# Prompt attention in groups of query blocks: scores, V products and transposes as runs of one shape, and PSUM split 3 and 5

## The chip, the cores and the metric

One core of a Trainium2 chip runs the whole program in one launch. The metric is the device time of one execution in microseconds (us); the kernel before takes 2353.92 us, the median of 3 runs (2352.94 to 2354.88).

## The reference, cut to what matters

One layer of a hybrid decoder is computed for a prompt of 1024 tokens and for 8 sample tokens. RMSNorm and one wide projection give the queries, keys and values of a dilated attention in three groups (windows 128, 512, 2048; dilations 1, 4, 16; 8 heads of 64), the inputs of an mLSTM, and gates. The two branches are gated, merged and projected; a convolutional FFN follows. The part that is changed is the prompt attention of one group:

```
def _dilated_attn_prompt(q, k, v, bias_g, window, dil):
    qb = to_blocks(q)                 # 128 queries of one residue modulo dil
    kb = with_prev(to_blocks(k))      # the block itself and the one before it
    vb = with_prev(to_blocks(v))
    s = jnp.einsum('brnqhc,brnkhc->brnhqk', qb, kb).astype(jnp.float32) * (Dh ** -0.5) + bias
    s = jnp.where(mask[None, None, :, None], s, -jnp.inf)
    lse = jax.nn.logsumexp(s, axis=-1)
    p = jnp.exp(s - lse[..., None]).astype(v.dtype)
    o = jnp.einsum('brnhqk,brnkhc->brnqhc', p, vb)
```

The outputs of the three groups are combined with weights from their log-sums. All data is float32.

## The kernel before, in words

The program runs in phases: norm and transposition of the input; attention (4 pairs of heads, for each the three groups g = 0, 1, 2: twelve units); the mLSTM, four heads; merging and output projection; the FFN. Large projections go through `proj` (L200) and `mm` (L183): a weight of 128 columns is split into a high and a low part (`split`, L175: ACT writes whi at L176, DVE writes wlo at L177), and for each of three token chunks 24 matmuls (L189) accumulate into a PSUM bank. These banks come from the pool `pp` (4 banks); ACT or DVE then empties the bank ("evacuation"). All other PSUM results come from the pool `px` (4 banks) by `X(...)`. Large SBUF tiles come from one pool, `ap_`, with NA = 17 buffers, by `A(...)`.

One attention unit (`attn_unit`, L324) projects q, k and v for 128 columns (two heads), transposes v and k (L365, tile ptr), writes the cache outputs, loads two bias tiles (bt), and goes through eight query blocks. For a block with a previous block nk = 2, else 1: in g = 0 all but the first have one (15 key blocks in all), in g = 1 every second (12), in g = 2 none (8). `stage_s(b)` issues the scores of the two heads, each into a bank of its own (L413, tile s; the heads lie on partitions 0 to 63 and 64 to 127, array shape 64\*128), then for each head a DVE pass that adds the bias and takes the row minimum (L420) and an ACT exponential (L424). `stage_t(b)` transposes the 2·nk blocks of probabilities into one bank (L434, tile pt, shape 128\*128) and copies it to SBUF (L436, tile pts; the planner picks DVE or ACT). `stage_v(b)` multiplies by the values (L451, tile po, shape 128\*64, the two heads on two halves of the columns); after four blocks the po bank is copied to oT (L459 or L463). The loop at L465 issues s of block x, t of block x-1, v of block x-2.

This is program order only. A planner that models time orders each engine's instructions: of what is ready in its model it takes what stands first in the program. So matmuls L189 of the next unit's projections fill places where the attention has to wait ("fillers" here). `in_order(m)` forbids that m moves ahead of the instruction traced before it on its engine; it doesn't forbid others between the two. At run time each engine's order is fixed; semaphores make it wait.

From the second pair on, the units also carry work of the pair before: `combine_b` and `sample_b` after g = 0, `combine_c` (L514) and `sample_c` after g = 1, `sample_d` after g = 2. `combine_c` loads factors (fbc, by the queue of POOL) and multiplies with them on DVE (L519, held in program order); `sample_c` multiplies small matrices on PE (L557, L562, L563), followed by DVE L565 and ACT L566. The gate projection L621 stands after the first unit.

Of the kernel before, what the change touches and what calls it, by code (L numbers as in the profile page):

```python
# [8 lines left out]
F32 = mybir.dt.float32  # L9
# [18 lines left out]
EPS = 1e-6  # L28
BIG = 1e30
NMC = 8  # L30
NA = 17
NF = 16
NC0 = 8

# [6 lines left out]
def kernel(  # L41
# [42 lines left out]

    wk = Phase()
    wk.next()
    pp = ctx.enter_context(tc.tile_pool(name="pp", bufs=4, space=bass.MemoryType.PSUM))
    px = ctx.enter_context(tc.tile_pool(name="px", bufs=4, space=bass.MemoryType.PSUM))

    def A(name, cols=T, dt=F32):  # L90
        return ap_.tile([128, cols], dt, tag="A", name=name)
# [6 lines left out]
    def X(name):  # L98
        return px.tile([128, 512], F32, tag="x", name=name)
# [224 lines left out]
    def attn_unit(pair, g, st):  # L324
        d = DIL[g]
        U = S // d
        qT, kT, vT = A("qT"), A("kT"), A("vT")
        evacs = []
        for kind, dst in enumerate((qT, kT, vT)):
            def evac(ci, t0, n, ps, kind=kind, dst=dst):  # L330
                npm = min(n, S - t0)
                if g == 0:
                    dv, sv = dst[:, t0:t0 + npm], ps[:, 0:npm]
                else:
                    dv = dst[:, 0:S].rearrange("p (r u) -> p r u", r=d)[:, :, t0 // d:(t0 + npm) // d]
                    sv = ps[:, 0:npm].rearrange("p (u r) -> p r u", r=d)
                if kind == 0:
                    nc.scalar.mul(dv, sv, -0.125)
                elif kind == 1:
                    nc.scalar.copy(dv, sv)  # L340
                else:
                    nc.vector.tensor_copy(dv, sv)  # L342
                if npm < n:
                    if kind == 0:
                        nc.vector.tensor_scalar(out=smp[:, pair, kind, g, :], in0=ps[:, npm:n], scalar1=-0.125, scalar2=None, op0=ALU.mult)
                    else:
                        nc.vector.tensor_copy(smp[:, pair, kind, g, :], ps[:, npm:n])
            col = kind * AQ + g * 512 + pair * 128
            if pair == 0 and g == 0 and kind < 2:
                evacs.append(evac)  # L350
                if kind == 1:
                    for ci in range(len(CHUNKS)):
                        for k in range(2):
                            proj_chunk(first_w[k], hT, evacs[k], ci)
            else:
                proj(w_in2[:, col:col + 128], hT, evac)
        vn = A("vn")
        kn = A("kn")
        keep = ((7,), (1, 3, 5, 7), tuple(range(8)))[g]
        for src, dst, blks in ((vT, vn, tuple(range(8))), (kT, kn, keep)):  # L360
            for b0 in range(0, len(blks), 4):
                bl = blks[b0:b0 + 4]
                pt = X("ptr")
                for i, b in enumerate(bl):
                    nc.tensor.transpose(pt[:, i * 128:(i + 1) * 128], src[:, b * 128:(b + 1) * 128], ident)  # L365
                if dst is vn or g != 1:
                    dv = dst[:, bl[0] * 128:(bl[-1] + 1) * 128]
                    sv = pt[:, 0:len(bl) * 128]
                else:
                    dv = dst[:, 0:S].rearrange("p (r n c) -> p r n c", n=2, c=128)[:, :, 1, :]  # L370
                    sv = pt.rearrange("p (r c) -> p r c", c=128)
                if dst is vn:
                    nc.vector.tensor_copy(dv, sv)
                else:
                    nc.scalar.copy(dv, sv)
        for kv, src in ((0, kn), (1, vn)):
            o = kvp[g][0, 0].rearrange("t k h c -> t k (h c)")[:, kv, pair * 128:(pair + 1) * 128]
            if g == 0:
                dma_out(o, src[:, 7 * 128:8 * 128])
            elif g == 1:  # L380
                dma_out(o.rearrange("(u r) c -> u r c", r=4), src[:, 0:S].rearrange("p (r n c) -> p r n c", n=2, c=128)[:, :, 1, :])
            else:
                ov = o.rearrange("(u j q) c -> q u j c", j=8, q=2)
                for q in range(2):
                    dma_out(ov[q], src[q * 64:(q + 1) * 64, 0:S].rearrange("p (j c) -> p j c", c=128))
        bias = []
        for hd in range(2):
            gh = g * 8 + pair * 2 + hd
            bt = wk.tile([128, 256], F32, tag="bias", name="bt", bufs=4)
            r, h0 = (0, 0) if gh < 2 else (1, 2) if gh < 8 else (g + 1, g * 8)  # L390
            base = (gh - h0) * 128 * 384
            if g < 2:
                dma_in(bt, _bcast(rep_d[r][:, :, :], base + 127, [[383, 128], [1, 256]]))
            else:
                dma_in(bt[:, 128:256], _bcast(rep_d[r][:, :, :], base + 255, [[383, 128], [1, 128]]))
                nc.gpsimd.memset(bt[64:128, 128:192], BIG)
            bias.append(bt)
        oT = A("oT")
        live = {}
        pos = [None, None]  # L400

        def span(b):
            prev = (g == 0 and b > 0) or (g == 1 and b % 2 == 1)
            nk = 2 if prev else 1
            return nk, b - (nk - 1)

        def stage_s(b):
            nk, k0 = span(b)
            kw = nk * 128
            ss_ = [X("s"), X("s")]  # L410
            for hd in range(2):
                pr = slice(hd * 64, (hd + 1) * 64)
                m = nc.tensor.matmul(ss_[hd][:, 0:kw], qT[pr, b * 128:(b + 1) * 128], kT[pr, k0 * 128:k0 * 128 + kw], start=True, stop=True)  # L413
                if hd:
                    in_order(m)
            for hd in range(2):
                sb = wk.tile([128, 256], F32, tag="sb", name="sb", bufs=4)
                cm = (g * 8 + b) * 4 + hd
                cl = (g * 8 + b) * 4 + 2 + hd
                nc.vector.tensor_tensor_reduce(  # L420
                    out=sb[:, 0:kw], in0=ss_[hd][:, 0:kw], in1=bias[hd][:, 256 - kw:256], scale=1.0, scalar=3e38,
                    op0=ALU.add, op1=ALU.min, accum_out=st[:, cm:cm + 1],
                )
                nc.scalar.activation(out=sb[:, 0:kw], in_=sb[:, 0:kw], func=ACTF.Exp, scale=-1.0, bias=st[:, cm:cm + 1], accum_out=st[:, cl:cl + 1])  # L424
                live[(b, hd)] = sb

        def stage_t(b):
            nk, _ = span(b)
            pt = X("pt")
            for hd in range(2):  # L430
                p = live.pop((b, hd))
                for i in range(nk):
                    c = (hd * nk + i) * 128
                    nc.tensor.transpose(pt[:, c:c + 128], p[:, i * 128:(i + 1) * 128], ident)  # L434
            pts = wk.tile([128, 512], F32, tag="pts", name="pts", bufs=3)
            nc.any.tensor_copy(pts[:, 0:nk * 256], pt[:, 0:nk * 256])  # L436
            live[b] = pts

        def stage_v(b):
            nk, k0 = span(b)  # L440
            pts = live.pop(b)
            half, bi = divmod(b, 4)
            if bi == 0:
                pos[half] = X("po")
            po = pos[half]
            for i in range(nk):
                kb = k0 + i
                for hd in range(2):
                    pr = slice(hd * 64, (hd + 1) * 64)
                    c = (hd * nk + i) * 128  # L450
                    m = nc.tensor.matmul(  # L451
                        po[pr, bi * 128:(bi + 1) * 128], vn[:, kb * 128 + hd * 64:kb * 128 + hd * 64 + 64],
                        pts[:, c:c + 128], start=(i == 0), stop=(i == nk - 1),
                    )
                    if hd or i:
                        in_order(m)
            if bi == 3:
                if g == 0:
                    nc.any.tensor_copy(oT[:, half * 512:(half + 1) * 512], po)  # L459
                else:  # L460
                    hr = d // 2
                    dv = oT[:, 0:S].rearrange("p (u r) -> p r u", r=d)[:, half * hr:(half + 1) * hr, :]
                    nc.any.tensor_copy(dv, po.rearrange("p (r u) -> p r u", r=hr))  # L463

        for x in range(8 + 2):  # L465
            if x < 8:
                stage_s(x)
            if 0 <= x - 1 < 8:
                stage_t(x - 1)
            if 0 <= x - 2 < 8:  # L470
                stage_v(x - 2)
        return oT

    def combine_a(pair, st):
# [975 lines left out]
```

## Time and profile before

| | before |
|---|---|
| median of 3 runs | 2353.92 us (2352.94 to 2354.88) |
| the profiled execution, its own time | 2352.78 us |
| its span, first to last instruction | 2350.9 us |
| PE (matmul) busy | 2321.8 us, 99% |
| DVE, ACT, POOL busy | 1161.4, 695.9, 212.3 us |
| granted TensorE clock, mean | 0.998 |
| attention phase, about | 67 to 667 us of the span |

In the timeline a row is a merged stretch of equal instructions: start, duration, engine, source line, operation, tiles, array shape (rows\*columns that the instruction uses), operand shape, count, and in brackets the idle time before it with what ended it. A float32 matmul shows as two records, a float32 transpose as one. PEld is the weight load.

### The profile page before, as it was taken

To read this page: it belongs to the slowest core of one execution; us is meant where nothing else is said; L and a number is where in the kernel's file an instruction comes from. 1 tells how busy PE (TensorE), PEld (TensorE's weight loads), DVE (VectorE), ACT (ScalarE), POOL (GpSimd) and SP (SyncE) were. 2 spreads that over 40 slices of the span, in tenths; PEclk is the share of its full clock that TensorE was granted. 3 is DMA by queue.
4 is the path that set the end of the run, shared out by engine and by line. 5 is a ranking of instruction groups with operands and counts; after the bars stand their busy time and mean duration, and the time that the engine had idled before them with its cause. 6 is when DMAs were issued, how large, how long until landed. Compare 5 with 4: busy or idle time off the path is not lost.

```text
span 2350.9 us, 36526 instructions
## 1 busy us (share of the span) xinstructions
PE 2321.8 (99%) x15077; PEld 2185.2 (93%) x15077; DVE 1161.4 (49%) x2697; ACT 695.9 (30%) x1345; POOL 212.3 (9%) x380
## 2 busy tenths in 40 slices
PE   7999999999999999999999999999999999999997
PEld 7888888888889999999999999999999999999997
DVE  6343434324345282827332254346556566655666
ACT  4333333333332332323332221333212222222222
POOL 1112111110120011111121200000000000000000
PEclk9999999999999999999999999999999999999999
DMA  5312433323354142424233631222111111111112
GB/s 175 100 51 75 116 84 89 97 68 95 99 164 130 43 136 59 133 62 133 61 119 88 218 114 46 69 85 63 37 45 44 39 54 54 55 45 38 53 37 77
DMA packets 243015, 196.82 MB, mean 84 GB/s; under 512 B 24392, under 2 KB 220088, under 8 KB 242833
## 3 DMA queue, kind: packets, MB, share of 16 engines
q1 hardware_dynamic: 206577, 124.65, 18.4%
q0 software_dynamic: 36272, 69.84, 9.7%
q8 instruction: 119, 1.95, 0.3%
q14 instruction: 47, 0.39, 0.1%
HBM read 160.30 MB, written 39.20 MB: 85 GB/s over the span
## 4 chain that ended last, share of the span: by engine, by line
PE 93%; issue 3%; DMA 2%; DVE 1%; ACT 1%; POOL 1%; DVEq 0%; SPq 0%; POOLq 0%; ACTq 0%
PE pp L189 67%; PE ppd L1343 10%; PE s L413 3%; PE po L451 2%; PE pt L434 2%; PE pcm L960 1%; PE ni L954 1%; DMA fbc<-f_d 1%; PE ptr L365 1%; PE sm L941 1%; PE na L957 1%; PE pxo L1211 1%; POOL out_dram L108 0%; DMA araw<-aT_d 0%; PE pkm L930 0%
## 5 line engine op out<-in xcount | busy, mean ns | idle before, releaser
L189 PE MATMUL pp<-act_hi,whi 128*128 128x352 f32 (+1 forms) x3272 | 604.8, 324 | 1.3 <-ACT act_hi L241 1.3
L189 PE MATMUL pp<-act_lo,whi 128*128 128x352 f32 (+1 forms) x3272 | 594.2, 321 | 0.0
L189 PE MATMUL pp<-act_hi,wlo 128*128 128x352 f32 (+1 forms) x3272 | 581.5, 319 | 1.1 <-DVE wlo L177 1.1
L189 PEld LDWEIGHTS pp<-act_hi,whi 128*128 128x128 f32 x3272 | 527.6, 188 | 14.6 <-issue 7.7
L189 PEld LDWEIGHTS pp<-act_lo,whi 128*128 128x128 f32 x3272 | 526.9, 188 | 5.8 <-issue 2.2
L189 PEld LDWEIGHTS pp<-act_hi,wlo 128*128 128x128 f32 x3272 | 524.2, 187 | 4.2 <-DVE wlo L177 1.4
L177 DVE TENSOR_TENSOR wlo<-wraw,whi 128x1024 fp32r<-128x1024 f32 (+2 forms) x153 | 182.0, 1190 | 457.8 <-PE pp L189 237.9
L176 ACT CAST whi<-wraw 128x1024 fp32r<-128x1024 f32 (+2 forms) x153 | 156.7, 1024 | 679.8 <-PE pp L189 627.3
L1344 DVE TENSOR_TENSOR x<-x,ppd 128x352 f32<-128x352 f32 (+4 forms) x248 | 124.8, 516 | 75.2 <-PE ppd L1343 75.1
L1269 DVE TENSOR_TENSOR fu<-pp,sq 128x320 f32<-128x320 f32 (+1 forms) x130 | 64.7, 511 | 182.0 <-PE pp L189 181.7
L1343 PE MATMUL ppd<-fhi,dhi 128*128 128x352 f32 (+3 forms) x528 | 124.2, 320 | 2.1 <-DVE yn L1304 2.1
L1343 PE MATMUL ppd<-flo,dhi 128*128 128x352 f32 (+3 forms) x528 | 123.7, 320 | 0.0
L1343 PE MATMUL ppd<-fhi,dlo 128*128 128x352 f32 (+3 forms) x528 | 123.7, 320 | 0.0
L1283 DVE SCALAR_TENSOR_TENSOR y<-fu,fcv,y 128x1048 f32<-128x1048 f32 x88 | 115.1, 1308 | 2.4 <-ACT y L1281 1.2
L424 ACT ACTIVATE sb<-sb,st 128x128 f32<-128x128 f32 (+1 forms) x192 | 85.2, 445 | 42.5 <-DVE st L420 41.4
L1343 PEld LDWEIGHTS ppd<-fhi,dhi 128*128 128x128 f32 x528 | 89.6, 188 | 3.9 <-issue 2.6
L1343 PEld LDWEIGHTS ppd<-flo,dhi 128*128 128x128 f32 x528 | 89.6, 188 | 1.3
L1343 PEld LDWEIGHTS ppd<-fhi,dlo 128*128 128x128 f32 x528 | 89.4, 188 | 1.4
L420 DVE CUSTOM_DVE_ANT_0 sb<-s,bt 128x128 f32<-128x128 f32 (+1 forms) x192 | 61.6, 350 | 51.3 <-PE s L413 41.5
L105 POOL DMA_DIRECT2D gfin<-in_final_norm_g_dram x1 | 0.5, 530 | 911.4 <-DVE fu L1269 911.4
L413 PE MATMUL s<-kT,qT 64*128 64x128 f32 (+1 forms) x384 | 70.8, 370 | 0.0
L342 DVE COPY vT<-pp 128x352 f32<-128x352 f32 (+1 forms) x36 | 18.5, 514 | 105.4 <-PE pp L189 105.4
(380 smaller groups left out, 2386.6 us busy)
## 6 DMA issues: line engine op xcount, KB each, us to landing
wraw<-in_w_in_dram SPq DMA_DIRECT2D x84, 512.0 KB
wraw<-in_w_up_dram SPq DMA_DIRECT2D x44, 512.0 KB
draw<-in_w_down_dram SPq DMA_DIRECT2D x22, 512.0 KB
c<-in_state_mlstm_C_dram SPq DMA_DIRECT2D x32, 256.0 KB
out_dram<-c POOLq DMA_DIRECT2D x32, 256.0 KB, 3.6
qb<-sn_d POOLq DMA_DIRECT2D x12, 512.0 KB, 5.1
kt<-in_cache_kv_w_dram SPq DMA_DIRECT2D x12, 512.0 KB
vt<-in_cache_kv_w_dram SPq DMA_DIRECT2D x12, 512.0 KB
```

The lines of the kernel that those rows point to most:

```text
L176: a = nc.scalar.copy(hi[:, 0:n], raw[:, 0:n])
L177: b = nc.vector.tensor_tensor(out=lo[:, 0:n], in0=raw[:, 0:n], in1=hi[:, 0:n].bitcast(F32), op=ALU.subtract)
L189: nc.tensor.matmul(ps[0:m, 0:n], wt[:, i * m:(i + 1) * m], act[i][which][:, t0:t0 + n], start=(pi == 0 and i == 0), stop=(pi == 2 and i == ...
L413: m = nc.tensor.matmul(ss_[hd][:, 0:kw], qT[pr, b * 128:(b + 1) * 128], kT[pr, k0 * 128:k0 * 128 + kw], start=True, stop=True)
L420: nc.vector.tensor_tensor_reduce(out=sb[:, 0:kw], in0=ss_[hd][:, 0:kw], in1=bias[hd][:, 256 - kw:256], scale=1.0, scalar=3e38, op0=ALU.add ...
L424: nc.scalar.activation(out=sb[:, 0:kw], in_=sb[:, 0:kw], func=ACTF.Exp, scale=-1.0, bias=st[:, cm:cm + 1], accum_out=st[:, cl:cl + 1])
L434: nc.tensor.transpose(pt[:, c:c + 128], p[:, i * 128:(i + 1) * 128], ident)
L451: m = nc.tensor.matmul(po[pr, bi * 128:(bi + 1) * 128], vn[:, kb * 128 + hd * 64:kb * 128 + hd * 64 + 64], pts[:, c:c + 128], start=(i == ...
L1269: nc.vector.tensor_tensor(out=u[:, 2 + t0:2 + t0 + npm], in0=ps[:, 0:npm], in1=r2[:, t0:t0 + npm], op=ALU.mult)
L1283: nc.vector.scalar_tensor_tensor(out=y, in0=u[:, i:i + YW], scalar=fcv3[:, i, j:j + 1], in1=y, op0=ALU.mult, op1=ALU.add)
L1343: nc.tensor.matmul(ps[:, 0:n], wds[j][w][:, m * 128:(m + 1) * 128], parts[j][a][:, t0:t0 + n], start=(x == 0), stop=(x == len(seq) - 1))
L1344: nc.vector.tensor_tensor(out=x1[m][:, t0:t0 + n], in0=x1[m][:, t0:t0 + n], in1=ps[:, 0:n], op=ALU.add)
```

## The change

Query blocks are taken in groups (`groups`, two blocks for g = 0 and 1, four for g = 2). Each stage takes a whole group: the scores of all its blocks go into two banks (one for each head, up to 512 columns), the transposes fill one or two banks of four, and V products follow each other; `chained` holds the matmuls of a stage in program order. Within the transposes the order is reversed, last block first. The loop issues s of group x, v of group x-2, t of group x-1 (V products now stand before the transposes). The bias pass and the exponential stay one for each block and head. PSUM is split 3 (`pp`) and 5 (`px`); sb has 8 buffers instead of 4, and NA is 16 instead of 17. Cut to its core:

```diff
-NA = 17
+NA = 16
...
-    pp = ctx.enter_context(tc.tile_pool(name="pp", bufs=4, space=bass.MemoryType.PSUM))
-    px = ctx.enter_context(tc.tile_pool(name="px", bufs=4, space=bass.MemoryType.PSUM))
+    pp = ctx.enter_context(tc.tile_pool(name="pp", bufs=3, space=bass.MemoryType.PSUM))
+    px = ctx.enter_context(tc.tile_pool(name="px", bufs=5, space=bass.MemoryType.PSUM))
...
+        G = 4 if g == 2 else 2
+        groups = [range(b, b + G) for b in range(0, 8, G)]
+
+        def chained(ms):
+            for i, m in enumerate(ms):
+                if i:
+                    in_order(m)
+
+        def stage_s(bs):
             ss_ = [X("s"), X("s")]
...
+            def matmuls():
+                for b in bs:
+                    nk, k0 = span(b)
+                    kw = nk * 128
+                    for hd in range(2):
+                        pr = slice(hd * 64, (hd + 1) * 64)
+                        yield nc.tensor.matmul(ss_[hd][:, at[b]:at[b] + kw], qT[pr, b * 128:(b + 1) * 128], kT[pr, k0 * 128:k0 * 128 + kw], start=True, stop=True)
+
+            chained(matmuls())
...
+                    sb = wk.tile([128, 256], F32, tag="sb", name="sb", bufs=8)
...
+        def stage_t(bs):
+
+            work = [(b, hd, i) for b in bs for hd in range(2) for i in range(span(b)[0])]
+            banks = [work[i:i + 4] for i in range(0, len(work), 4)]
+            pts = {}
+
+            def matmuls():
+                for bank in reversed(banks):
+                    pt = X("pt")
+                    for x, (b, hd, i) in reversed(list(enumerate(bank))):
+                        yield nc.tensor.transpose(pt[:, x * 128:(x + 1) * 128], live[(b, hd)][:, i * 128:(i + 1) * 128], ident)
+                    t = wk.tile([128, 512], F32, tag="pts", name="pts", bufs=3)
+                    n = len(bank) * 128
+                    nc.any.tensor_copy(t[:, 0:n], pt[:, 0:n])
...
+            chained(matmuls())
...
+        def stage_v(bs):
+            pts = live.pop(bs)
+
+            def matmuls():
+                for b in bs:
...
+                    for i in range(nk):
+                        kb = k0 + i
+                        for hd in range(2):
+                            pr = slice(hd * 64, (hd + 1) * 64)
+                            yield nc.tensor.matmul(
+                                po[pr, bi * 128:(bi + 1) * 128], vn[:, kb * 128 + hd * 64:kb * 128 + hd * 64 + 64],
+                                pts[(b, hd, i)], start=(i == 0), stop=(i == nk - 1),
+                            )
+
+            chained(matmuls())
...
-        for x in range(8 + 2):
-            if x < 8:
-                stage_s(x)
-            if 0 <= x - 1 < 8:
-                stage_t(x - 1)
-            if 0 <= x - 2 < 8:
-                stage_v(x - 2)
+        n = len(groups)
+        for x in range(n + 2):
+            if x < n:
+                stage_s(groups[x])
+            if 0 <= x - 2 < n:
+                stage_v(groups[x - 2])
+            if 0 <= x - 1 < n:
+                stage_t(groups[x - 1])
```

## Rows read from the trace of the kernel before

**Rows 1.** The profile's page, part 1: busy time, share, instructions.

```profile
PE 2321.8 (99%) x15077; PEld 2185.2 (93%) x15077; DVE 1161.4 (49%) x2697; ACT 695.9 (30%) x1345; POOL 212.3 (9%) x380
```

**Rows 2.** Timeline of PE, steady stretch of g = 0.

```profile
237.02 0.70 PE L413 MATMUL s<-kT,qT 64*128 64x256 f32 x4
237.66 0.66 PE L434 MATMUL pt<-ident,sb 128*128 128x128 f32 x4
238.24 0.66 PE L451 MATMUL po<-pts,vn 128*64 128x128 f32 x8
238.83 0.70 PE L413 MATMUL s<-kT,qT 64*128 64x256 f32 x4
```

**Rows 3.** Timeline of PE: longer and shorter stretches.

```profile
96.09 1.09 PE L451 MATMUL po<-pts,vn 128*64 128x128 f32 x16
...
286.70 0.44 PE L434 MATMUL pt<-ident,sb 128*128 128x128 f32 x2
...
287.65 0.49 PE L413 MATMUL s<-kT,qT 64*128 64x128 f32 x4
...
297.28 0.83 PE L557 MATMUL psb<-ohs,rbx 33*16 33x129 f32 x6
```

**Rows 4.** Windows (units): length; PE, PEld, DVE, ACT, POOL busy (x); clock; DMA.

```profile
227.95:245.15 17.20, 17.11 (x131) 10.46 (x130) 12.11 (x52) 10.60 (x37) 3.96 (x8) 1.00 0.73 216
279.47:299.65 20.18, 20.02 (x132) 12.09 (x132) 9.57 (x40) 11.39 (x38) 6.48 (x9) 1.00 0.80 198
334.33:349.05 14.72, 14.72 (x99) 9.29 (x98) 7.53 (x42) 9.46 (x38) 5.21 (x8) 1.00 0.51 127
```

**Rows 5.** Timeline of DVE, then ACT: one block's softmax and copy.

```profile
239.67 0.42 DVE L420 CUSTOM_DVE_ANT_0 sb<-s,bt 128x256 f32<-128x256 f32 x1 [0.43 <-PE s L413]
...
240.37 0.69 DVE L436 COPY pts<-pt 128x512 f32<-128x512 f32 x1
...
240.14 0.51 ACT L424 ACTIVATE sb<-sb,st 128x256 f32<-128x256 f32 x1 [0.24 <-DVE st L420]
```

**Rows 6.** Timeline: start of the program, and the first unit.

```profile
37.92 0.32 PE L189 MATMUL pp<-act_hi,whi 128*128 128x352 f32 x1
...
43.02 0.59 PE L189 MATMUL pp<-act_hi,wlo 128*128 128x352 f32 x2
...
42.38 0.47 ACT L338 ACTIVATE qT<-pp 128x352 f32<-128x352 f32 x1
...
79.74 1.45 PE L189 MATMUL pp<-act_hi,whi 128*128 128x352 f32 x8
...
91.35 0.56 DVE L621 TENSOR_SCALAR gsb<-pp,gb_sb 8x352 f32<-8x352 f32 x1
```

**Rows 7.** Timeline at the end of g = 1, second and third pair.

```profile
281.95 2.52 POOL L105 DMA_DIRECT2D fbc<-f_d  x3
...
301.83 2.36 DVE L519 TENSOR_TENSOR oT<-oT,fbc 128x1024 f32<-128x1024 f32 x2 [6.27 <-DMA fbc<-f_d]
...
462.12 2.36 DVE L519 TENSOR_TENSOR oT<-oT,fbc 128x1024 f32<-128x1024 f32 x2 [9.46 <-DMA fbc<-f_d]
...
464.98 0.62 ACT L566 ACTIVATE ssb<-ssb,s 16x387 f32<-16x387 f32 x1 [8.07 <-DVE s L565]
...
465.60 0.79 ACT L338 ACTIVATE qT<-pp 128x352 f32<-128x352 f32 x2
...
466.22 1.44 PE L189 MATMUL pp<-act_hi,whi 128*128 128x352 f32 x8
```

**Rows 8.** Timeline of PE, then DVE, in the FFN.

```profile
1632.72 1.45 PE L189 MATMUL pp<-act_hi,whi 128*128 128x352 f32 x8
...
1640.16 0.48 PE L1343 MATMUL ppd<-fhi,dhi 128*128 128x352 f32 x2
...
1633.68 1.25 DVE L1316 TENSOR_TENSOR y<-y 128x1048 f32<-128x1048 f32 x1
...
1638.40 0.52 DVE L1269 TENSOR_TENSOR fu<-pp,sq 128x352 f32<-128x352 f32 x1
```

More of the change, by code (lines that the diff above doesn't have):

```diff
@@ L405, in span @@
             return nk, b - (nk - 1)
-        def stage_s(b):
-            nk, k0 = span(b)
-            kw = nk * 128
-            ss_ = [X("s"), X("s")]
[L411 to L447, printed above, removed]
-                for hd in range(2):
[L449 to L453, printed above, removed]
-                    )
-                    if hd or i:
-                        in_order(m)
-            if bi == 3:
+        G = 4 if g == 2 else 2
@@ new lines, in attn_unit @@
+        groups = [range(b, b + G) for b in range(0, 8, G)]
[4 more added lines that the diff above has]
+        def stage_s(bs):
+            ss_ = [X("s"), X("s")]
+            at, c = {}, 0
+            for b in bs:
+                at[b] = c
+                c += span(b)[0] * 128
+            def matmuls():
[6 more added lines that the diff above has]
+            chained(matmuls())
+            for b in bs:
+                kw = span(b)[0] * 128
+                for hd in range(2):
+                    sb = wk.tile([128, 256], F32, tag="sb", name="sb", bufs=8)
+                    cm = (g * 8 + b) * 4 + hd
+                    cl = (g * 8 + b) * 4 + 2 + hd
+                    nc.vector.tensor_tensor_reduce(
+                        out=sb[:, 0:kw], in0=ss_[hd][:, at[b]:at[b] + kw], in1=bias[hd][:, 256 - kw:256], scale=1.0, scalar=3e38,
+                        op0=ALU.add, op1=ALU.min, accum_out=st[:, cm:cm + 1],
+                    )
+                    nc.scalar.activation(out=sb[:, 0:kw], in_=sb[:, 0:kw], func=ACTF.Exp, scale=-1.0, bias=st[:, cm:cm + 1], accum_out=st[:, cl:cl + 1])
+                    live[(b, hd)] = sb
@@ new lines, in stage_t @@
+        def stage_t(bs):
[10 more added lines that the diff above has]
+                    nc.any.tensor_copy(t[:, 0:n], pt[:, 0:n])
+                    for x, w in enumerate(bank):
+                        pts[w] = t[:, x * 128:(x + 1) * 128]
+            chained(matmuls())
+            for b in bs:
+                for hd in range(2):
+                    live.pop((b, hd))
+            live[bs] = pts
@@ new lines, in stage_v @@
+        def stage_v(bs):
+            pts = live.pop(bs)
+            def matmuls():
+                for b in bs:
+                    nk, k0 = span(b)
+                    half, bi = divmod(b, 4)
+                    if bi == 0:
+                        pos[half] = X("po")
+                    po = pos[half]
+                    for i in range(nk):
+                        kb = k0 + i
+                        for hd in range(2):
+                            pr = slice(hd * 64, (hd + 1) * 64)
[4 more added lines that the diff above has]
+            chained(matmuls())
+            for b in bs:
+                half, bi = divmod(b, 4)
+                if bi < 3:
+                    continue
+                po = pos[half]
```

## The prediction

> **What bounds the kernel now.** The page's first part shows PE busy 99% of the span, DVE 49%, ACT 30% [rows 1]: the end is set by what PE spends, and a microsecond that PE is spared is gained as long as PE finds other work ready. I then read the timeline of PE through the attention, where the rows are shortest. In a steady stretch of g = 0 one block's s, t and v take 1.81 us (237.02 to 238.83) [rows 2]. How much of this is work? Rows of the same kind and different length tell: 128 columns more lengthen four score records by 0.70 - 0.49 = 0.21; two transposes more add 0.66 - 0.44 = 0.22, so 0.11 each; eight V records more add 1.09 - 0.66 = 0.43, so 0.054 each [rows 2, 3]. Work is then 0.42 + 0.44 + 0.43 = 1.29, and 0.52 is left, paid once for each stretch of one array shape: some 0.17 at every change between 64\*128, 128\*128 and 128\*64. That is what the reader is to see: PE is busy all the time, yet 0.52 of 1.81 us is no work.
>
> The windows over three units of the second pair say what this sums to. Each window runs from the first scores to the projection behind the last V product: 17.20, 20.18 and 14.72 us [rows 4]. Work by the prices above: g = 0 has 15 key blocks, so 15 x 0.21 for s, 30 transposes x 0.11, 60 V records x 0.054, in all 9.7 us; g = 1 has 12, 7.75; g = 2 has 8, 5.2. In the timeline of PE I counted 9, 13 and 11 filler matmuls at 0.155 (48 of them from 1632.72 to 1640.16 [rows 8]), 1.4, 2.0 and 1.7 us, and small matmuls of the sample tokens, none, 15 and 6 at about 0.12 (0.83 / 6 with its tail [rows 3]), 1.8 and 0.7. What is left is 6.1, 8.6 and 7.1 us. The same timeline has 30, 41 and 38 stretches of one shape: 0.2 each. g = 1 and 2 have more than three for a block, because the planner alternates single transposes with pairs of V records.
>
> **The change part by part.** *Groups, chained.* g = 0 and 1 go from eight trios of stretches to four, g = 2 to two: 10 trios per pair x 0.52 = 5.2 us. Fillers beside transposes have their shape and cost no change; I allow three per unit that do, 0.2 each: 1.8. The sample matmuls keep their own changes, some 1.8 in g = 1 and 2. Sum 8.8 in place of 21.8: 13 per pair, by unit 3.4, 4.9 and 4.7, and 52 over four pairs. The first unit has fewer changes than its fellows (25 stretches from 66.9 to 97.1), so I take 50. The work itself, the passes on DVE and ACT and the DMAs with their queues (SP, POOL) stay as they are.
>
> *Softmax of a group.* This isn't shown before; I build it from rows. The first pass of DVE may have to wait for the last score of the group, as it reads the bank that PE still writes. Two passes take 0.70 on DVE, an exponential 0.5 on ACT, a copy 0.69 [rows 5]. In g = 0 a group needs 4 x 0.35 + 2 x 0.69 = 2.8 of DVE and 4 x 0.5 = 2.0 of ACT against 2 x 1.29 + 0.52 = 3.1 of PE, and from s of a group to its t there is s, v, t of neighbours in between, some 4 us for a chain of 0.14 + 0.35 + 2.0 + 0.2. So it is hidden in the steady part. V of a group now comes right behind one s run of 4 x 0.21 + 0.17 = 1.0 us after the transposes it needs: two copies on two engines (0.69 and a wait) are done by then, on one engine (1.4) they would show 0.4 in each of 40 groups, 16 us at most. At either end of a unit the planner must put fillers; they are the same matmuls as before. Cost taken: nothing; if the fillers don't fit, see the first rival.
>
> *px from 4 to 5.* Two s banks, two pt, one po: one group fits. A gain that I can't price beyond the above; zero.
>
> *pp from 4 to 3.* It bites where a fourth chunk runs before the first is emptied. At the start a fourth chunk runs from 37.92 to 43.02 while the first bank is emptied only at 42.38 [rows 6]; with three banks nearly its whole 24 x 0.155 = 3.7 us moves behind. In the first unit a fourth chunk starts at 79.74 behind three gate chunks that are emptied from 91.35 on [rows 6]; it fills up to 3.8 us in which the attention waits for its softmax. Bounds 0 (if the planner empties sooner) to 7.5; the rows show both holes, so I take 5. In the FFN a chunk that ends where the next eight matmuls begin, at 1632.72, is emptied by 1638.40 + 0.52 = 1638.92, and with three banks it would be due at 1640.16 [rows 8]: 1.2 us of room, cost nothing.
>
> *NA from 17 to 16, sb from 4 to 8.* In the second pair three loads fbc are issued together [rows 7], so several buffers are free where most tiles live at once; cost nothing, upper bound the 0.155 x 24 = 3.7 us of one chunk per pair that can't be emptied, 15.
>
> *What the shorter units run into.* The fbc loads are issued at the start of g = 1 (281.95) and land 20 us later; DVE, in order, sits idle for them 6.27 us in the second pair and 9.46 in the third [rows 7]. They will not land sooner. Behind the waiting L519 stand DVE's L565, behind that ACT's L566 (8.07 us idle), behind that the evacuation L338 of the next q chunk, done near 466.05; PE starts its fourth chunk at 466.22 [rows 7]. With three banks that start can't be earlier: in the third pair the 4.9 us of g = 1 are given back whole. In the other two pairs the idle is 3.2 us shorter, and 1.7 each is given back: 8.3 in all. If the planner puts L565 ahead of L519, since psc is ready sooner, nothing is. Bounds 0 to 3 x 4.9 = 14.7; I take 4, half of 8.3.
>
> **The sum.** -50 + 5 + 4 = -41 us. The profiled execution took 2352.78 us (its span 2350.9), the median of the runs 2353.92, 1.1 more. 2353.9 - 41 = 2313 us.
>
> **The rivals.** *Softmax sets the pace* (2328). DVE and ACT are busy 12.1 and 10.6 of 17.2 us in g = 0 [rows 4]. If no filler fits between a group and its neighbours, a unit lasts as long as its chain: first s 1.1, pass and wait 0.5, then 16 exponentials of 0.5 (g = 0), then t, copy, v 2.7: 12.3 us. With 0.4 for half the columns, an estimate, g = 1 comes to 10.8 and g = 2 to 10.6. Sum 33.7 against 52.1 - 5.1 (fillers, done elsewhere) - 2.5 (sample) = 44.5: 10.8 less per pair, 43; 1 us of latency at each of twelve seams leaves 31. With the holes at the start 2353.9 - 31 + 5 = 2328. For it: DVE is at 70% already. Against: PE was never without fillers. The Trainium skill says the same in TensorEngine Tiling (Array Packing), section PSUM Bottleneck: tiles speed TensorE up, not the emptying of PSUM, and copies may become the bottleneck. The windows don't bear it out yet: no unit is as short as its DVE time.
>
> *The factors hold the attention itself* (2347). If the planner also puts the last pts copies of g = 1 on DVE behind L519, PE's last V products wait until fbc has landed: from 279.47 to 301.8, three multiplications 3.6, copy 0.7, V 1, so 28 us for 20.2, in three pairs 23.4 lost instead of 14.7 gained. 2313 - 4 + 38 = 2347. Against: before, ACT did such copies in that place.
>
> *The runs are split again* (2338). `chained` forbids moving ahead, not standing between; if one of two s banks is late, or the planner puts fillers inside, half of the saved changes return: 25.
>
> *Slower, by the FFN* (2370). The 22 second-half projections have 1.2 us of room [rows 8]. If DVE's order slips by three passes of 1.25 us (L1316 [rows 8]) ahead of the evacuation, each waits 3.75 - 1.2 = 2.6 us, 57 in all: 2313 + 57 = 2370. It decides from a slip of 1.2 us on, and makes the kernel slower from 3.1 us on (41 / 22 + 1.2). For it: DVE is busiest there. Against: the planner knows of the three banks.
>
> **How the numbers follow.** Forecast 0.52 (2313, by itself 2302 to 2325); better, with neither holes nor factors, 0.12 (2304); softmax 0.12; factors 0.06; split again 0.08; nothing changes, since splits and holes eat all, 0.04; slower by the FFN 0.06. From no change a measurement can tell some 0.2%, 4.7 us. So faster 0.90, same 0.04, slower 0.06. The range goes from 2299 (all of the 52, px worth 3 more) to 2338.
>
> **What would show it.** The timeline of a unit of g = 0 should have s rows of eight records, t of eight, V of 16, some 15 to 18 stretches; the windows of the three units should be near 14, 15.5 and 10 us with as many fillers, and a pair's period 13 us shorter. Holes of 3 us should stand near 40 and 80 us. DVE's idle before L519 should grow to some 10 to 14 us. I am wrong if PE has idle rows inside the units, if stretches stay near 100 per pair, or if the projections in FFN or mLSTM lose pace (0.155 per matmul).

## The result, and the profile after

The changed kernel takes 2314.91 us (median of 4 runs, 2312.85 to 2316.65) against 2353.43 (4 runs, 2350.08 to 2354.88): ratio 0.9838, 95% interval 0.9821 to 0.9855, 38.5 us less. The forecast was 2313, 41 less. The profiled execution took 2312.85 us, its span is 2311.0, 39.9 below the span before. It is the fastest of the four.

Part 1 of the page after answers to [rows 1]; PE has lost 57 us of busy time with the same number of instructions, and 1% of its share:

```profile
PE 2264.6 (98%) x15077; PEld 2174.5 (94%) x15077; DVE 1152.1 (50%) x2689; ACT 686.6 (30%) x1337; POOL 211.4 (9%) x380
```

The timeline of PE in the steady part of g = 0, second pair, answers to [rows 2]:

```profile
229.36 1.09 PE L455 MATMUL pt<-ident,sb 128*128 128x128 f32 x8
230.38 1.14 PE L429 MATMUL s<-kT,qT 64*128 64x256 f32 x8
231.48 1.09 PE L482 MATMUL po<-pts,vn 128*64 128x128 f32 x16
232.51 1.09 PE L455 MATMUL pt<-ident,sb 128*128 128x128 f32 x8
233.36 1.05 PE L189 MATMUL pp<-act_lo,whi 128*128 128x352 f32 x5
234.73 1.09 PE L482 MATMUL po<-pts,vn 128*64 128x128 f32 x16 [0.32 <-ACT pts L458]
```

Two blocks now take 3.15 us for transposes, scores and V products (229.36 to 232.51), where they took 2 x 1.81. Each row has twice the records of before and one change of shape as before. The rows also show that it is the change of shape that costs, and not the start of another kind of matmul: the scores come 1.02 us behind the start of eight transposes (229.36 to 230.38), fillers, which have the shape of the transposes, 0.85 (232.51 to 233.36). The difference is 0.17.

The windows of the three units of the second pair, from the first scores to what follows the last V product, answer to [rows 4] (columns: length; PE, PEld, DVE, ACT, POOL busy with counts; granted clock; DMA share; GB/s):

```profile
222.59:238.60 16.01, 14.87 (x141) 11.78 (x140) 13.87 (x58) 9.79 (x36) 4.30 (x9) 1.00 0.73 219
271.40:286.01 14.61, 14.30 (x134) 10.78 (x134) 9.27 (x41) 10.53 (x37) 6.47 (x9) 1.00 1.01 216
322.03:334.25 12.22, 11.40 (x112) 10.22 (x111) 5.42 (x35) 9.43 (x38) 5.18 (x8) 1.00 0.65 153
```

In the timeline I counted 13, 13 and 5 stretches of one shape in these windows, and 17, 14 and 31 fillers. By the prices of the prediction their work is 12.3, 11.7 and 10.0 us; 3.7, 2.9 and 2.2 are left, 8.8 in all, where 8.8 were forecast and 21.8 stood before. With 8, 12 and 12 fillers as in the windows before (the prediction's 9, 13 and 11 are off by one each, which changes nothing) the units would take 14.6, 14.3 and 9.3 us, near the 14, 15.5 and 10 that it gave as a sign. The 8.8 aren't made of what was forecast, though. These rows, the first transposes of the three units, show waits for the last exponential of their group:

```profile
226.68 0.87 PE L455 MATMUL pt<-ident,sb 128*128 128x128 f32 x6 [0.81 <-ACT sb L442]
...
275.10 0.88 PE L455 MATMUL pt<-ident,sb 128*128 128x128 f32 x6 [0.31 <-ACT sb L442]
...
326.89 1.09 PE L455 MATMUL pt<-ident,sb 128*128 128x128 f32 x8 [0.82 <-ACT sb L442]
```

With 0.32 more at 234.73, where V products wait for the copy of their probabilities, the units hold 2.3 us of waits, which the forecast put at nothing, and 6.5 of changes, which it put at 8.8.

What each part of the run gave (starts of the first scores of a unit, from the timeline; the second pair begins at 227.95 before and 222.59 after):

| part | before | after | difference |
|---|---|---|---|
| start, to the first scores | 66.9 | 68.0 | +1.1 |
| first unit, to the scores of the second | 61.1 | 65.7 | +4.7 |
| rest of the first pair | 100.0 | 88.9 | -11.1 |
| second pair | 157.1 | 145.0 | -12.2 |
| third pair | 157.2 | 143.6 | -13.6 |
| fourth pair, without its last unit | 106.4 | 98.5 | -7.9 |
| last unit, to the end | 1702.3 | 1701.3 | -0.9 |

The savings are where they were forecast, 13 to 14 us in a clean pair. The first two lines and the last are where PE stands idle. The first line is at its smallest here: in the profiles of the other kernels at 3 and 5 the first scores come at 69.7 to 71.0 us, with the lower clock behind the first hole lasting longer. Near 40 and 80 us, where PE now waits with three full banks (answers to [rows 6]):

```profile
40.15 0.63 PE L238 MATMUL pxt<-ident,xn 8*128 8x8 f32 x8 [2.51 <-DVE xn L229]
...
84.60 1.54 PE L455 MATMUL pt<-ident,sb 128*128 128x128 f32 x6 [3.48 <-ACT sb L442]
86.07 2.08 PE L429 MATMUL s<-kT,qT 64*128 64x256 f32 x8
```

and the windows around them (the column before the DMA share is the granted clock):

```profile
40.00:45.00 5.00, 4.85 (x22) 3.11 (x23) 3.27 (x10) 1.45 (x5) 1.66 (x3) 0.76 0.17 46
45.00:50.00 5.00, 5.00 (x31) 5.00 (x30) 0.00 (x0) 0.46 (x1) 4.37 (x4) 0.90 0.31 65
81.00:84.60 3.60, 0.12 (x1) 0.00 (x0) 3.38 (x16) 3.21 (x11) 0.00 (x0) 0.85 0.23 53
84.60:88.00 3.40, 3.40 (x14) 2.33 (x14) 1.45 (x4) 1.92 (x8) 0.00 (x0) 0.50 0.33 98
```

The holes have the forecast length, 2.5 and 3.5 us. But behind the second one PE runs at a granted clock of 0.50, the lower of its two levels, 1.2 GHz, until about 90: eight score records that take 1.14 in the steady part take 2.08 here. This wasn't in the sum. A third hole was in no part of it. At the end of the attention PE waits for products of the sample tokens (`sc`, DVE L578), and two rows of fillers behind it take nearly double their 1.44:

```profile
644.79 0.28 PE L598 MATMUL psc<-ident,sc 128*16 128x128 f32 x1 [0.53 <-DVE sc L578]
...
647.74 0.38 PE L598 MATMUL psc<-ident,sc 128*16 128x128 f32 x1 [2.54 <-DVE sc L578]
...
648.20 2.71 PE L189 MATMUL pp<-act_hi,whi 128*128 128x352 f32 x8
650.71 2.55 PE L189 MATMUL pp<-act_lo,whi 128*128 128x352 f32 x8
```

The factors behave as forecast. One row of each engine, in the order of the chain; they answer to [rows 7]:

```profile
273.86 2.51 POOL L105 DMA_DIRECT2D fbc<-f_d  x3
...
293.89 1.23 DVE L555 TENSOR_TENSOR oT<-oT,fbc 128x1024 f32<-128x1024 f32 x1 [12.26 <-DMA fbc<-f_d]
...
295.62 0.62 ACT L602 ACTIVATE ssb<-ssb,s 16x387 f32<-16x387 f32 x1 [9.45 <-DVE s L601]
...
296.24 0.78 ACT L338 ACTIVATE qT<-pp 128x352 f32<-128x352 f32 x2
...
296.73 1.55 PE L189 MATMUL pp<-act_hi,whi 128*128 128x352 f32 x8 [1.41 <-ACT qT L338]
```

DVE is idle 12.26 us before the first multiplication, ACT behind it, then the evacuation of q; PE's fourth chunk comes 1.41 late. In the third pair DVE's idle is 10.92 and PE loses 0.08, in the fourth 11.42 and 0.58.

### The profile page after: what moved, and what is told of

It is laid out like the page before. It is cut to its first block, busy times and chain, and to the rows that moved or that the text cites. A ratio compares the mean times of both kernels' runs of the same rounds, so it can differ in the third digit from the quotient of the medians.

```text
span 2311.0 us, 36395 instructions
## 1 busy us (share of the span) xinstructions
PE 2264.6 (98%) x15077; PEld 2174.5 (94%) x15077; DVE 1152.1 (50%) x2689; ACT 686.6 (30%) x1337; POOL 211.4 (9%) x380
## 4 chain that ended last, share of the span: by engine, by line
PE 84%; DMA 5%; issue 3%; ACT 2%; DVE 1%; POOL 1%; DVEq 0%; POOLq 0%; ACTq 0%
PE pp L189 64%; PE ppd L1379 10%; DMA fbc<-f_d 3%; PE pcm L996 1%; ACT sb L442 1%; PE ni L990 1%; PE po L482 1%; PE pt L455 1%; PE s L429 1%; PE na L993 1%; PE sm L977 1%; PE pxo L1247 1%; PE ptr L365 0%; POOL out_dram L108 0%; PE pkm L966 0%
## 5 line engine op out<-in xcount | busy, mean ns | idle before, releaser
L189 PE MATMUL pp<-act_hi,whi 128*128 128x352 f32 (+1 forms) x3272 | 598.5, 324 | 4.4 <-ACT qT L338 2.0
L189 PE MATMUL pp<-act_lo,whi 128*128 128x352 f32 (+1 forms) x3272 | 585.2, 320 | 0.0
L1317 ACT ACTIVATE y<-fu,fcv 128x1048 f32<-128x1048 f32 x44 | 55.7, 1266 | 30.3 <-DVE fu L1307 30.0
L438 DVE CUSTOM_DVE_ANT_0 sb<-s,bt 128x128 f32<-128x128 f32 (+1 forms) x192 | 54.8, 347 | 17.4 <-PE pt L455 8.7
```

Source lines behind the costliest of these rows:

```text
L189: nc.tensor.matmul(ps[0:m, 0:n], wt[:, i * m:(i + 1) * m], act[i][which][:, t0:t0 + n], start=(pi == 0 and i == 0), stop=(pi == 2 and i == ...
L438: nc.vector.tensor_tensor_reduce(out=sb[:, 0:kw], in0=ss_[hd][:, at[b]:at[b] + kw], in1=bias[hd][:, 256 - kw:256], scale=1.0, scalar=3e38, ...
L1317: nc.scalar.activation(out=y, in_=u[:, 0:YW], func=ACTF.Identity, scale=fcv3[:, 0, j:j + 1], bias=fcv3[:, 3, j:j + 1])
```

## The experiments

Times are medians; the ratio is to runs of the kernel before on the same chip, whose median was 2350.3 to 2354.7. After stands at 0.9838.

### One block per group

```diff
-        G = 4 if g == 2 else 2
+        G = 1
```

> One block per group, all else as after: same matmuls, same banks, same stage order s, v, t, still chained. The built order of PE has 349 stretches of one array shape in the attention, against 130 after and 422 before. Theory (a change of shape costs 0.17 us, and nothing else matters): 219 more changes, +37 us, so 2315 + 37 = 2352, no faster than before by more than some 2 us. Rival (the gain comes from the other stage order or from px = 5, so that softmax is hidden better): most of the gain stays, 2315 to 2325. The trios should take 1.8 us in place of 3.15 for two blocks.

Measured: 2338.48, ratio 0.9939 (0.9924 to 0.9953): 24 us of the gain go. The time lies between the theory's and the rival's. Timeline of PE, steady part of g = 0:

```profile
235.86 0.70 PE L429 MATMUL s<-kT,qT 64*128 64x256 f32 x4
236.71 0.66 PE L482 MATMUL po<-pts,vn 128*64 128x128 f32 x8 [0.15 <-DVE pts L458]
237.30 0.66 PE L455 MATMUL pt<-ident,sb 128*128 128x128 f32 x4
237.89 0.70 PE L429 MATMUL s<-kT,qT 64*128 64x256 f32 x4
```

A block takes 2.03 us: 1.81 as before, and V waits some 0.2 for the copy, since only one score run stands between. A pair takes 151.7 with 95 and 93 stretches, against 143.6 with 39 in the third pair of after. That is 54 x 0.15 = 8.1 a pair, close to the theory; without PE's idle time, 2.4 us of the pair in after and 1.1 here, it is 0.17 each. The total was overstated, since this kernel has none of the waits of after at the first transposes (1.9 of the 2.3 per pair) and none at the factors or in the tail. So the grouping carries most of the gain; stage order and buffers without it leave 14 of 38 us.

`chained` itself makes no difference: without its `in_order` the planner puts out the same order on every engine, instruction by instruction. It is the grouping in program order that the planner follows.

### The kernel before with the buffers of after

```diff
-NA = 17
+NA = 16
...
-    pp = ctx.enter_context(tc.tile_pool(name="pp", bufs=4, ...))
-    px = ctx.enter_context(tc.tile_pool(name="px", bufs=4, ...))
+    pp = ctx.enter_context(tc.tile_pool(name="pp", bufs=3, ...))
+    px = ctx.enter_context(tc.tile_pool(name="px", bufs=5, ...))
...
-                sb = wk.tile([128, 256], F32, tag="sb", name="sb", bufs=4)
+                sb = wk.tile([128, 256], F32, tag="sb", name="sb", bufs=8)
```

> The kernel before with the buffers of after alone: PSUM 3 and 5, NA 16, sb 8. Its built order of PE has 399 stretches of one shape in the attention, 23 fewer than before. Theory: 23 x 0.17 = 4 us gained, up to 5 lost in holes of 2.5 and 3.5 us near 40 and 80 us: 2352 to 2357 against 2353.4. Rival (the buffers themselves make the gain, as px = 5 takes waits out of the attention): 2320 to 2335. Rival (pp = 3 costs more, as chunks in the FFN or mLSTM wait for their bank): over 2360, with PE idle in those phases.

Measured: 2349.63, 0.9984 (0.9975 to 0.9994), somewhat better than the theory. The first scores come 2.9 us later than before and those of the second unit 7.0, by the same holes (2.28 and 2.11 us of idle PE). Against that a pair takes 155.0 instead of 157.1, with 110 and 108 stretches instead of 116 and 114. So the new buffers are worth 2 us a pair in the old order, where I had put zero; the run doesn't part the fifth px bank from the larger sb. In the FFN there is no new idle PE, and a wait of 1.97 us near the end of the program is gone; at 729 us, ahead of the mLSTM, PE waits 2.10 us where it waited 1.10.

### After with PSUM split 4 and 4

```diff
-    pp = ctx.enter_context(tc.tile_pool(name="pp", bufs=3, ...))
-    px = ctx.enter_context(tc.tile_pool(name="px", bufs=5, ...))
+    pp = ctx.enter_context(tc.tile_pool(name="pp", bufs=4, ...))
+    px = ctx.enter_context(tc.tile_pool(name="px", bufs=4, ...))
```

> After with PSUM split 4 and 4 again, all else as after. The built order of PE has 138 stretches, 8 more. Theory: 8 x 0.17 = 1.4 us lost, the holes near 40 us (2.5) and 80 us (3.5) and the wait before the fourth chunk behind g = 1 (1.4 and 0.7) filled, 8 us back: 2308 to 2312, unless four banks of px make groups wait for each other. Rival (a group needs its five banks: two s, two pt, one po): each of 40 groups waits some 0.5 us for a bank, +20, 2325 to 2335, with idle rows of PE before s or t.

Measured: 2307.22, 0.9807 (0.9792 to 0.9821). The theory holds, 0.8 us below its range, the rival doesn't: a pair takes 144.3, and four px banks serve the groups nearly as well as five. The windows that answer to those around the holes:

```profile
40.00:45.00 5.00, 5.00 (x27) 2.71 (x27) 3.46 (x10) 1.90 (x6) 1.02 (x2) 1.00 0.08 21
45.00:50.00 5.00, 5.00 (x36) 5.00 (x34) 1.30 (x2) 1.49 (x2) 4.30 (x6) 1.00 0.30 68
80.00:83.00 3.00, 3.00 (x26) 2.44 (x26) 2.24 (x10) 2.72 (x12) 0.00 (x0) 1.00 0.58 166
```

No hole, and the clock at 1.00. The first scores of the second unit come at 123.7, in after at 133.7. The two holes and what hangs on them thus cost 10 us between these two kernels. Not all of it is the change's: the kernel before, without a hole, had a dip of the clock of its own there (0.61 in the window 46 to 50), so what set it off at this place stays open.

### Groups of two in g = 2

```diff
-        G = 4 if g == 2 else 2
+        G = 2
```

> Groups of two blocks instead of four in g = 2, all else as after. 152 stretches against 130. Theory: 22 x 0.17 = 3.7 us more, 2318.6. Rival (the shape changes are cheap when fillers stand between, or the softmax chain of a group of four is what holds g = 2): no difference or faster, 2311 to 2315.

Measured: 2311.32, 0.9828 (0.9814 to 0.9843): not slower, as the rival said, but for another reason than its own. The units of g = 2 do last longer, 46.2 and 46.3 us to the next first scores instead of 45.5 and 45.6: six more changes, less the 0.6 by which the wait before the first transposes is shorter (0.22 for 0.82 in the third pair). What makes up for it lies in the tail. From the first scores of the last unit to the V product of the last sample step, after takes 54.6 us and this kernel 48.8, for the same matmuls: it has no wait for `sc` there and a granted clock of 1.00 in that window, after 0.94. So the third hole costs after some 6 us, 3.1 of waiting and the rest at the lower clock.

### Transposes in forward order

```diff
-                for bank in reversed(banks):
+                for bank in banks:
...
-                    for x, (b, hd, i) in reversed(list(enumerate(bank))):
+                    for x, (b, hd, i) in enumerate(bank):
```

> After with the transposes of a group in forward order (first block first), all else as after. The built order of PE has 157 stretches in the attention against 130: the V products are now split by others. Theory one (the reversal is there to keep V runs whole, and a change costs 0.17): 27 more changes, +4.6, 2319.5. Theory two (reversed, the first transpose of a unit waits for the last exponential of its group, 0.3 to 0.8 us in each of twelve units; forward it waits for the first): up to 7 back, 2312. Both together: 2314 to 2317, with no idle PE before the transposes and more rows of V.

Measured: 2315.85, 0.9850 (0.9835 to 0.9864), no difference from after that can be told. The transposes start with the first exponential, but in g = 0 and 1 PE has nothing between scores and transposes in the planner's order and waits all the same, 0.93 and 0.41; only in g = 2 the wait falls, from 0.82 to 0.1 and splinters of 0.06. And then runs are split: a pair has six changes more than in after and takes 145.3 to 145.7 us, against 143.6 to 145.0. So theory one has the direction. The equal total has other reasons: the first scores come 3.0 us later, the wait for `sc` is missing in the tail, and from the first scores of the last unit to the end it takes 3.9 us less (1697.4). Timeline of PE, first transposes of g = 0 in the second pair:

```profile
228.29 0.33 PE L455 MATMUL pt<-ident,sb 128*128 128x128 f32 x1 [0.93 <-ACT sb L442]
228.38 0.40 PE L189 MATMUL pp<-act_hi,whi 128*128 128x352 f32 x1
228.67 0.33 PE L455 MATMUL pt<-ident,sb 128*128 128x128 f32 x1
```

### Stages in the order s, t, v

```diff
-            if 0 <= x - 2 < n:
-                stage_v(groups[x - 2])
             if 0 <= x - 1 < n:
                 stage_t(groups[x - 1])
+            if 0 <= x - 2 < n:
+                stage_v(groups[x - 2])
```

> After with the loop issuing s, t, v as the kernel before did, in place of s, v, t. 135 stretches against 130. Theory (the order of the three stages is worth only its changes): +0.9, within noise of after, 2314 to 2317. Rival (V products have to stand behind the next scores, or they wait for their copies, 0.4 in each of 40 groups): 2325 to 2331, with idle PE before V.

Measured: 2325.66, 0.9897 (0.9881 to 0.9914). The rival has the number right and the cause wrong: V waits nowhere for its copies. PE waits 1.6 to 3.6 us behind g = 1 in three pairs, at the factors. On POOL's queue their loads now stand behind a store of the softmax sums, which waits for an exponential: in the fourth pair they are issued at 577.19, 10.5 us behind the first scores of their unit, in after at 562.35, 2.5 behind, and DVE sits idle 14.61 us for them. The next run shows the same. The three holes sum to 6.9 of the 10 us; no run has this order of stages with the loads first, so that the queue makes all of it is not shown.

### The sample's step ahead of the factors

```diff
-                combine_c(*done)
                 sb = sample_c(done[0], sc)
+                combine_c(*done)
```

> After with the sample tokens' step c traced ahead of the step that multiplies by the factors. PE's order is unchanged; on DVE the sample's pass (L601) now stands ahead of the first multiplication that waits for the factors. Theory (the holes of 1.41 us at 295 and 0.73 at 583 come from DVE standing at the factors, with the evacuation of q behind it on ACT): both holes go, ACT's wait of 8 to 9 us before its L602 goes, 2 us gained, 2313. Rival (the holes come from three pp banks alone): the holes stay, 2315.

Measured: 2325.27, 0.9891 (0.9876 to 0.9906), 10 us slower; the theory fell, and the rival with it. POOL, DVE and PE in the fourth pair:

```profile
577.06 0.71 POOL L108 DMA_DIRECT2D stn_d<-st  x1 [1.12 <-ACT sb L442]
577.69 2.49 POOL L105 DMA_DIRECT2D fbc<-f_d  x3
...
580.51 0.55 DVE L601 CUSTOM_DVE_ANT_0 ssb<-psc,ssb 16x387 f32<-16x387 f32 x1 [4.59 <-ACT oT L498]
593.98 1.23 DVE L555 TENSOR_TENSOR oT<-oT,fbc 128x1024 f32<-128x1024 f32 x1 [11.55 <-DMA fbc<-f_d]
...
601.66 2.56 PE L189 MATMUL pp<-act_hi,whi 128*128 128x328 f32 x8 [4.38 <-DVE smp L345]
604.01 2.39 PE L189 MATMUL pp<-act_lo,whi 128*128 128x328 f32 x8
```

L601 is early, as meant. But the loads of the factors are now issued at 577.69, behind the stores, 12.0 us behind the first scores of their unit instead of 2.5, and DVE's next wait for them holds another evacuation, that of the sample columns (L345). PE stands 4.38 us, and its next sixteen matmuls take 4.54 us instead of some 2.4, at a granted clock of 0.50. Two readings were left: the place of the loads in POOL's queue, or the place of L601 on DVE. The next run tells them apart.

### The same with the loads first

```diff
-                combine_c(*done)
+                fb = load_c(done[0])
                 sb = sample_c(done[0], sc)
+                combine_c(*done, fb)
```

(`load_c` issues the three loads, `combine_c` only multiplies.)

> As sample_first, but the three loads of the factors are traced ahead of the sample's step c and only the multiplications behind it. On POOL's queue the loads stand again ahead of the stores of the softmax sums (stn_d), as in after; on DVE the sample's pass stays ahead of the first multiplication. Theory from sample_first (its 10 us came from the loads that were issued 13 to 15 us later, behind a store that waits for the last exponential): they are issued 5 us behind the start of the unit again, the holes of 2.0, 2.2 and 4.6 us shrink to 0 to 1.5, 2311 to 2315 with before at 2353.4. Rival (the place of the sample's pass on DVE is what costs, as the multiplications now hold another evacuation): the holes stay, 2322 or more.

Measured: 2311.76, 0.9822 (0.9806 to 0.9838). POOL and DVE in the fourth pair (lines behind 550 are 7 higher here):

```profile
562.25 2.49 POOL L105 DMA_DIRECT2D fbc<-f_d  x3
...
574.62 0.55 DVE L608 CUSTOM_DVE_ANT_0 ssb<-psc,ssb 16x387 f32<-16x387 f32 x1 [4.59 <-ACT oT L498]
582.23 3.50 DVE L562 TENSOR_TENSOR oT<-oT,fbc 128x1024 f32<-128x1024 f32 x3 [5.68 <-DMA fbc<-f_d]
```

The loads are issued at 562.25 again, 2.5 us behind the first scores of the unit, the sample's pass runs 7.6 us ahead of the factors, and PE has no hole behind g = 1 in any pair. POOL's queue was the cause; with the loads in place the reordering on DVE is a gain of about 3 us by the medians, which the intervals, as they overlap, don't show; the three pairs with factors are 1.7, 0.4 and 0.8 shorter than in after.

### The 4 and 4 split with another tail

```diff
     gate_a(1)
-    sb = sample_c(3, sc)
     gate_a(2)
-    sample_d(3, *sb)
+    sb = sample_c(3, sc)
     gate_a(3)
+    sample_d(3, *sb)
```

> The 4 and 4 split, with the last sample step c moved behind the third gate projection and step d behind the fourth, so that PE doesn't wait in the tail of the attention for the sample's products. In the 4 and 4 run PE waits there 1.67 and 2.36 us. Theory (a hole in PE is time, as nothing else has slack): both go, 2307.2 - 4.0 = 2303. Rival (the tail is held by other loads, and what is moved waits later): 2306 to 2308.

Measured: 2300.31, 0.9785 (0.9770 to 0.9799), 5 us below the 4 and 4 run by the ratios, 7 by the medians. Timeline of PE, the place of the wait for `sc`:

```profile
646.43 0.28 PE L598 MATMUL psc<-ident,sc 128*16 128x128 f32 x1
...
647.32 0.20 PE L599 MATMUL psc<-ones,qk 128*16 128x1 f32 x2
647.45 1.56 PE L189 MATMUL pp<-act_hi,whi 128*128 128x352 f32 x8
```

No wait, and the fillers behind are at full speed (1.56 for eight with the change).

### The reversal in V instead of in the transposes

```diff
-                for bank in reversed(banks):
+                for bank in banks:
...
-                for b in bs:
+                for b in reversed(bs):
```

(on top of the run before; forward within a bank as well, and the po bank taken ahead of the loop)

> The 4 and 4 split with the tail as in b44_tail, and the reversal moved from the transposes to the V products: transposes run first block first, V products last block first. 165 stretches against 138. Theory (a change costs 0.17, and the wait before the first transposes of each of twelve units, 0.8 now, goes or shrinks as the first exponential releases them): +4.6 and -4 to -9, so 0.9785 of before shifts by 0 to -0.002. Rival (the waits only move, as in forward): 4 to 5 us slower than b44_tail, 0.980 to 0.981.

Measured: 2314.26, 0.9832 (0.9817 to 0.9847), a miss, worse than even the rival: 14 us lost. PE still waits 0.2 to 0.9 us before the first transposes of a unit, and the units of g = 1 take 51.4 instead of 49.7, their runs split. A pair is 2 us longer and the last unit with what follows 2.3, with a wait of 2.08 us for other products of the sample (`so`); that makes the 10 us between the two profiles, while the medians lie 14 apart.

### Both mends at 3 and 5, and at 4 and 4

> After, PSUM 3 and 5 as it is, with the two mends that do not touch PSUM: loads of the factors and the sample's pass as in loads_first, the tail as in b44_tail. Theory (each hole of PE costs its own length and the half clock behind it, and nothing else remains): the tail gives 5 to 6 (3.1 of waiting and about 2.7 at half clock), the factors 2 to 3, so 2306 to 2308 with before at 2353.4; what is then left against mended_4_4 are the holes near 40 and 80 us, 6 to 10 us. Rival (the tail's gain in b44_tail came from the fourth bank): 2311.

> b44_tail with the loads of the factors and the sample's pass as in loads_first. With four pp banks PE showed no hole at the factors. Theory: no difference to b44_tail, 2299 to 2303. Rival (the factors still cost something in shifted evacuations): 2 to 3 us faster.

Measured: 2304.99, 0.9790 (0.9776 to 0.9805) at 3 and 5, 1 us below the theory's range; 2302.25, 0.9780 (0.9764 to 0.9797) at 4 and 4. The tail's gain doesn't need the fourth bank: from the first scores of the last unit to the end it is 7.0 us at 3 and 5 (1693.9 against 1700.9 with the loads first alone) and 6.0 at 4 and 4 (1698.8 with another tail against 1704.8). At 4 and 4 the factors were no cost, as expected. At 3 and 5 the scores of the second unit come 11.9 us later (135.5 against 123.6), but a pair is 1.0 us shorter (143.2 against 144.2), and the 1.97 us for which PE waits near the end of the program at 4 and 4, as it did before, are missing. So the two splits end within 3 us of each other, and the intervals can't part them. Either beats both kernels of this case, and after by 10 to 13 us.

## Why the prediction was right

*The price of a change of shape* held, and with it the forecast. The changes went from 114 to 39 in the third pair and took 13.6 us along, 0.18 each; by the steps between, 0.26 each from before to single blocks (21 changes, 5.5 us) and 0.15 from there to after (54, 8.1; 0.16 against the mended kernel's 143.2). Why those of before were dearer isn't settled. The Trainium skill has a rule for this, in TensorEngine Tiling (Array Packing), section Key Properties: a change of the tiling mode drains TensorE, a change of tile within a mode does not. The timelines here agree, with some 0.17 us at a change between scores, transposes and V products, and none between transposes and fillers.

*The softmax of a group: nothing.* That step was wrong, in a small way. The first transposes of each unit wait 0.3 to 0.8 us, as a reversed group needs its last exponential first, and V products of g = 0 0.3 for a copy; 2.3 us per pair, some 9 in all. It didn't show since the planner made fewer stretches than I allowed (13, 13 and 5). Two errors of some 2 us a pair cancel, and that is luck. The rival in which softmax sets the pace isn't borne out: DVE is busy 13.87 of 16.01 us in g = 0, closer to it than before, but PE has other work.

*pp from 4 to 3: 5 us, at most 7.5.* Mis-sized. The holes came where they were forecast, at the forecast length. But the term was the length of the holes alone, and PE came out of the second at 0.50 of its clock. The first unit took 4.7 us longer although it has 12 fewer stretches (13 for 25, some 2 us); with the 1.1 at the start that is some 8 against before, and 10 against the same kernel at 4 and 4, above my upper bound.

*px from 4 to 5: zero.* Too low: about 1 us a pair with groups, by the mended pair of runs, and at most 2 in the old order, where sb grew with it. The split also has a part far from the attention. Near the end of the program PE waits for the final norm; in before, and for the same 1.97 us in each run at 4 and 4,

```profile
2334.15 0.71 PE L1343 MATMUL ppd<-fhi,dhi 128*128 128x256 f32 x4 [1.97 <-DVE yn L1304]
```

and in none of the nine kernels at 3 and 5, after among them. These 2 us were in no part of the sum.

*The factors: 4 us of 0 to 14.7.* Measured 2.1, by the chain that was named (DVE, L601, ACT, L338, PE) and with DVE's idle at 11 to 12 us in the forecast 10 to 14. That it stayed this low hung on the place of three loads in POOL's queue; behind the stores, with the sample's step first, they cost the kernel 10. My rival for this place looked at copies on DVE, not at that queue.

*The tail* had no term. The last unit should have given some 5 us, for 30 fewer stretches (20 for 50 to the last V product of the sample); the wait of 3.1 us and the lower clock behind it took back 6. With the 2 us at the end of the program, which came with the split, this makes the 0.9 of the table.

*The FFN and the mLSTM* kept their pace, and no wait of PE over 0.5 us is new in after; the slower rival didn't come.

In sum: 54 us of savings in the attention (2, 11.1, 13.6, 13.6, 8.5 and 5 in the units' rows of the table, before what was given back) where I had taken 50, and 16 given back in four places where I had taken 9 in three; with the 2 us at the end this is the 40 of the spans. That the total came so near to 41 is luck in part: 7 us too little in the costs stand against 4 too little in the savings and 2 that had no term. The split, which the forecast had as a small cost, was the weaker half of the change: the groups alone, at 4 and 4, give more.

## What to carry to other kernels

Where PE is the bound, count the stretches of one array shape: at 0.15 to 0.2 us each, 300 changes were 50 us that the busy share showed as work. Price a hole in PE by its length and by the granted clock of the window behind it, which can double it. And when a step is reordered, look where its loads fall in the issuing engine's queue: loads that a program line moved behind a waiting store came some 10 us later in their unit and cost more than the reordering could give.

## What the runs showed of the hardware

Behind the longer holes PE ran at a granted clock of 0.50, 1.2 GHz, for some 4 to 6 us: after those of 3.48 us at 81 to 84.6 and of 2.54 at 645 to 647.7 in after, and of 4.38 at 597 to 601.7 in the run with the sample's step first. Eight matmuls of 352 columns then take 2.6 to 2.7 us in place of 1.44. Behind the 1.41 us at the factors the clock stayed at 1.00.

The length of the hole alone doesn't tell whether the clock falls. Behind the 1.97 us near the end of the program it stayed at 1.00 in before and in the kernel with both mends at 4 and 4, and went to 0.50 (the stretch from 2 to 4 us behind) in the 4 and 4 split and in that split with another tail. Nor does the fall last equally long: behind the hole near 40 us the first scores came at 68.0 in after and at 71.0 with the transposes forward, where the clock was 0.50 from 40.2 to 48.2. I had not expected a hole to cost nearly twice its length; how the clock is decided the runs don't show.
